# Where the products on the samples' states, memories and last cached values stand in TensorE's order

## The chip, the cores and the metric

The kernel runs on one core of one Trainium2 chip. A core has TensorE (matrix products, results into PSUM banks), VectorE, ScalarE, GpSimd and SyncE, which issues most transfers. Each engine works through its own queue in order, and an instruction waits at the head of its queue until what it needs is done. The metric is the time of one execution on the device in microseconds (us), lower is better; a kernel's time is the median of several executions.

## The reference

One inference step of one decoder layer, for two groups of tokens that share all weights: a prompt of 512 tokens and a group of samples, 8 sequences with 8 new tokens each (64 tokens). Cut to what matters here:

```
u = rms(x) * g;  proj = u @ w_in                    # z, x/B/C, dt, q, k, v, gates, og
# 1. Mamba2 scan, 16 heads in 2 groups, state h (64 x 128 per head and sequence)
y   = C.B^T-weighted sum over the new tokens  +  exp(cum) * (C @ h0)
h1  = exp(cum_last) * h0 + sum_s w_s x_s B_s
# 2. mLSTM scan, 4 heads, memory c (128 x 256) and n (128)
num = (q.k^T * D) @ v  +  s_inter * (q @ c0)
c1  = scale * c0 + sum_s w_s k_s v_s
x   = x + rms(concat(y, h_ml) @ w_out) * g
# 3. cross-attention over 256 memory rows; samples use cached keys and values
o   = softmax(q @ k_mem^T / 16) @ v_mem;  x = x + rms(o @ w_xo) * g
# 4. SwiGLU
x   = x + rms((silu(u @ w_gate) * (u @ w_up)) @ w_down) * g
```

The prompt starts from zero states. Each of the 8 samples brings its own `h0` (16 heads of 64 x 128), `c0` (4 heads of 128 x 257 with n as the last column) and cached keys and values (256 x 4 x 256 each). So `C @ h0`, `q @ c0`, `q @ k_mem^T` and `p @ v_mem` of the samples are different small products for every sample, with 8 tokens each, while everything else runs over all 576 tokens together. Outputs are both groups' tokens and all new states and memories.

## The kernel before

All data is laid out with features on the 128 partitions and tokens along the columns. A weight tile is split into a high and a low part, and each product with it is three TensorE instructions (high with high, high with low, low with high; lines 215, 216 and 218, result tiles `ps_in`, `ps_xo` and so on). Plain float32 products, such as all products on states, are two instructions each in the trace.

The order of the work on each engine is made ahead of time by a scheduler: of the instructions whose inputs it holds to be ready, it puts next the one that stands first in the program. Two constructs bend this. `with tc.issue_after(x)` puts the block's instructions of x's engine behind x in that engine's order, without a wait of its own. `with tc.high_priority(offset=3000)` lets the block's instructions go as though they stood 3000 places earlier in the program. Once made, the order is fixed, and on the chip nothing passes an instruction that waits.

The small products of the samples use a part of the array. Four samples of 8 tokens make 32 columns of the stationary operand (`cpad` and `qpad` hold one sample's 8 columns and zeros beside them), so one product fills 32 of the 128 output partitions; four products into the four quarters of one bank run side by side. The trace shows these as `128*32`, and ordinary ones as `128*128`. Products with a 64-wide stationary operand show as `128*64`. Below, a "visit" is an unbroken run of `128*32` or `32*32` instructions between two full ones.

Three places have them.

*States (lines 804 to 828).* After the prompt's scan (`ssd_prompt(0)`, `ssd_prompt(1)`) stands the samples' scan. For b = 0 to 3 the loop loads the states of samples b and 4+b into two tiles `h0` (of four, tag `t4`), multiplies them with `cpad` into the bank `psh` (line 813, tile `ps_hs`, four products over two sequences and two groups), and then, for each of the two: GpSimd scales the state in place (line 821), two products `ps_hu` make the update (line 824), VectorE adds it (line 825, collected in `added`), and SyncE stores the state (line 827). `psh` takes one of the two banks of pool `pb`, `ps_hu` the other, until `yin` (line 829) has read `psh`. Around this in time stand products of the prompt's scan: `ps_yi` (line 710; `inner[0]` to `inner[3]` are the last ones of group 0's four tiles, `inner[4]` to `inner[7]` those of group 1) and `ps_h` (line 680, `states[0]` to `states[7]`), and as filling the input projection `ps_in` and the values' projection `ps_v` (line 882). The `ps_v` products follow a list written by hand: number n is put behind a given product of the scan, the first behind `inner[2]`, those from number 133 (counted from 0) behind `states[7]`, those from 159 behind `inner[4]`. The low parts of the first two `wv` units are put behind `added[0]` in VectorE's order.

*Memories (lines 1037 to 1059).* For each half of the samples (`hb`), bank `psn` takes four products of the new tokens (line 1042, `32*32`) and then, sample by sample, a loaded `c0` (four tiles) is multiplied with `qpad` (line 1049, tile `ps_nh`, four products each), updated by `ps_cu` (line 1056) and stored. The prompt's mLSTM heads (`ps_n`, line 983) run at the same time.

*Cached values (lines 1631 to 1651 and 1663 to 1678).* `pick` is a generator: it loads eight tiles of a half's cached keys or values (two per sample, line 1627, into `kv`, four tiles at the end), multiplies each with the samples' queries or weights (line 1640; `ps_sa` for keys, `ps_os` for values), 16 products for a pair of samples in one bank, and yields between its two pairs. `sample_step(m)` runs the next part with its TensorE instructions behind m. The last use, values of the first half, falls into the loop over `xo(j, 0)`, the first half of the attention's output projection: tiles j = 0, 1, 2 do their first six of eight steps (`step(0, KT - 2)`), then the last two steps behind the last products of the prompt's attention. Those last products are `ps_ov` (lines 1612 to 1614), whose results are split by ScalarE and VectorE (lines 202 and 203) into the tiles `oh` and `ol` (the trace names them `qh` and `ql`) that the last two steps read. The first pair stands at j = 1 with no tie, the second behind tile 4. Tiles 0, 1 and 2 hold all three banks of pool `pg`, and tile 3 needs one of them back.

Of the kernel before, what the change touches and what calls it, by code (L numbers as in the profile page):

```python
# [11 lines left out]
F32 = mybir.dt.float32  # L12
# [7 lines left out]
P = 128  # L20
# [95 lines left out]
def build(nc, tc, ctx, I, O):  # L116
# [686 lines left out]
    psh = BP("ps_hs")  # L803
    added = []
    hbs = [stacks(sd, btk.rearrange("p g k -> p (g k)"), xes.rearrange("p h k -> p (h k)"), hb, 2) for hb in range(2)]
    for b in range(4):
        hns = [sd.tile([P, 16, 64], F32, name="h0", tag="t4", bufs=4) for _ in range(2)]
        for hb in range(2):
            S.dma_start(hns[hb], I["h0"][4 * hb + b])
        for g in range(2):  # L810
            for hb in (1, 0):
                q = 32 * (2 * g + hb)
                mm(psh[q:q + 32, :], cpad[:, g, 4 * hb + b, :],
                   hns[hb][:, 8 * g:8 * g + 8, :].rearrange("p h k -> p (h k)"),
                   start=b == 0, stop=b == 3, skip_group_check=True)
        for hb in range(2):
            bb, hn, (bst, xst) = 4 * hb + b, hns[hb], hbs[hb]
            bm = sd.tile([96, 256], F32R, name="bm", tag="bm", bufs=1)
            A.activation(bm, bst.bitcast(F32), AF.Copy, scale=C32("bmask")[:96, b:b + 1])
            with tc.issue_after(mults[7].ins) if b == 2 else ExitStack():  # L820
                G.tensor_tensor(hn, hn, decs[:, :, bb:bb + 1].to_broadcast([P, 16, 64]), op=ALU.mult)
            for g in range(2):
                ps = BP("ps_hu")
                mm(ps, bm[:, g * P:(g + 1) * P], xst[:, g * 512:(g + 1) * 512], start=True, stop=True)
                added.append(V.tensor_tensor(hn[:, 8 * g:8 * g + 8, :], hn[:, 8 * g:8 * g + 8, :],
                                             ps.rearrange("p (h k) -> p h k", h=8), op=ALU.add))
            S.dma_start(O["ssms"][bb], hn.rearrange("p h k -> p (h k)"))
# [106 lines left out]
    def head_norm(num, ex, n4, pool, jk):  # L934
# [19 lines left out]
        V.tensor_tensor(a, a, d, op=ALU.mult)  # L954
        return a

    for h in range(4):
        q, k = qk[:, h, :], qk[:, 4 + h, :]
        psb = MP("ps_d")
        mm(psb, sel[:68, h:h + 1].to_broadcast([68, P]), sxst[:, 0:TP], start=True, stop=True)  # L960
        qs = mp_.tile([P, 384], F32, name="qs", tag="qs", bufs=2)
        A.activation(qs, psb[:, P:TP], AF.Exp)
        G.tensor_tensor(qs, qs, q[:, P:TP], op=ALU.mult)
        dm = mp_.tile([P, 512], F32, name="dm", tag="dm", bufs=2)
        for c in range(4):
            V.scalar_tensor_tensor(dm[:, c * P:(c + 1) * P], psb[:, c * P:(c + 1) * P], CT[:, c, 64 + h:65 + h],
                                   C16("maskp"), op0=ALU.add, op1=ALU.add)
        A.activation(dm, dm, AF.Exp)
        pss = MP("ps_s")
        for c in range(4):  # L970
            mm(pss[:, c * P:(c + 1) * P], k[:, c * P:(c + 1) * P], q[:, c * P:(c + 1) * P], start=True, stop=True,
               skip_group_check=True)
        V.tensor_tensor(dm, dm, pss, op=ALU.mult)
        psk = MP("ps_k")
        for c in range(4):
            TE.transpose(psk[:, c * P:(c + 1) * P], k[:, c * P:(c + 1) * P], ident)
        kw = mp_.tile([P, 4, P], F32, name="kw", tag="kw", bufs=2)
        V.tensor_tensor(kw, psk.rearrange("p (c k) -> p c k", c=4), wendm[:, 0:4, h:h + 1].to_broadcast([P, 4, P]),
                        op=ALU.mult)
        num = mp_.tile([P, 4, 257], F32, name="num", tag="num", bufs=2)  # L980
        for c in range(4):
            psn = MP("ps_n")
            mm(psn[:, 0:257], dm[:, c * P:(c + 1) * P], vt[c][:, h, 0:257], start=True, stop=c == 0)
            if c:
                mm(psn[:, 0:257], qs[:, (c - 1) * P:c * P], cprev[:, 0:257], start=False, stop=True)
            V.tensor_copy(num[:, c, :], psn[:, 0:257])
            psc = MP("ps_c")
            mm(psc[:, 0:257], kw[:, c, :], vt[c][:, h, 0:257], start=True, stop=True)
            cn = mp_.tile([P, 258], F32, name="cst_", tag="cst_", bufs=4)
            if c == 0:  # L990
                A.copy(cn[:, 0:257], psc[:, 0:257])
            else:
                V.scalar_tensor_tensor(cn[:, 0:257], cprev[:, 0:257], scalem[:, c, h:h + 1], psc[:, 0:257],
                                       op0=ALU.mult, op1=ALU.add)
            cprev = cn
        f = head_norm(num, expnm[:, :, h:h + 1].rearrange("p c o -> p (c o)"), 4, mp_,
                      mp_.tile([P, 256], F32, name="hn_jk", tag="hn_jk", bufs=1))
        S.dma_start(O["cp"][:, h, :], cprev[:, 0:257])
        for c in range(4):
            scaled = V.tensor_scalar(num[:, c, 0:256], num[:, c, 0:256], f[:, c:c + 1], None, op0=ALU.mult)  # L1000
        for dv in range(2):
            pst = MP("ps_ht")
            for c in range(4):
                ht = TE.transpose(pst[:, c * P:(c + 1) * P], num[:, c, dv * P:(dv + 1) * P], ident)
            htc = A.copy(qk[:, 4 * dv + h, 0:TP], pst)
# [26 lines left out]
    for h in range(4):  # L1032
        TE.transpose(psk[:TS, h * P:(h + 1) * P], qk[:, 4 + h, TP:T], ident)
    kws = ms.tile([TS, 4, P], F32, name="kws")
    V.tensor_tensor(kws, psk[:TS, :].rearrange("p (h k) -> p h k", h=4),
                    wendm[:TS, 4, :].unsqueeze(2).to_broadcast([TS, 4, P]), op=ALU.mult)
    for hb in range(2):
        r = slice(32 * hb, 32 * hb + 32)
        kst, vst = stacks(ms, kws.rearrange("p h k -> p (h k)"), vts.rearrange("p h k -> p (h k)"), hb)
        psn = BP("ps_nh")  # L1040
        for h in range(4):
            mm(psn[32 * h:32 * h + 32, 0:257], ds_[r, h, r], vt[4][r, h, 0:257], start=True, stop=False,
               tile_position=(32 * hb, 32 * h), skip_group_check=True)
        for b in range(4):
            bb = 4 * hb + b
            c0 = ms.tile([P, 4, 258], F32, name="c0", tag="t4", bufs=4)
            S.dma_start(c0, I["c0"][bb])
            for h in range(4):
                mm(psn[32 * h:32 * h + 32, 0:257], qpad[:, h, bb, :], c0[:, h, 0:257], start=False, stop=b == 3,
                   skip_group_check=True)  # L1050
            km = ms.tile([96, 512], F32R, name="km", tag="km", bufs=1)
            A.activation(km, kst.bitcast(F32), AF.Copy, scale=C32("bmask")[:96, b:b + 1])
            cn = c0
# [725 lines left out]
    for j in range(8):  # L1779
        step = xo(j, 0, wx if 3 < j < 7 else None)  # L1780
        if j < 3:

            step(0, KT - 2)
            with tc.issue_after(ends[-1].ins) if j else ExitStack():
                ends.append(step(KT - 2, KT)[0])
        else:
            ends.append(step(0, KT)[0])

        if j == 1:
            next(steps, None)  # L1790
        elif j == 4:
            sample_step(ends[-1])
    kxs.close()
    u3l = SL(5, "u3l", F32R)
# [847 lines left out]
```

## Time and profile before

| | |
|---|---|
| median of 3 executions | 1073.94 us (1070.35 to 1074.08) |
| the profiled execution, its own time | 1071.59 us |
| its span, first to last instruction | 1069.8 us |
| TensorE busy | 1060.1 us, 99% |
| VectorE, ScalarE, GpSimd busy | 775.2, 616.5, 236.9 us |
| HBM read and written | 162.11 and 20.65 MB |
| granted TensorE clock | 0.999 |

The profile is of one execution. TensorE instructions overlap one another: an instruction's duration reaches past the start of the next, so the time that a product costs is read from start to start, not from its duration. A row of the timeline gives the start and the duration in us, engine, line, operation, tiles (output and inputs), shapes and the count of instructions merged into it, and in brackets the idle time before it and what ended that. A row of the chain of waits gives the start, the length and the work.

### The profile page before, as it was taken

The page shows a single profiled execution, that of the slowest core. Times are in us where ns is not written, and L with a number is a line of the kernel's source. Part 1 is how long each engine was busy: PE and PEld are TensorE (multiplying, and loading weights), DVE is VectorE, ACT ScalarE, POOL GpSimd, SP SyncE. Part 2 cuts the span into 40 slices and gives each one's busy share as a digit, 9 for nine tenths or more (in the row PEclk, how much of TensorE's full clock was granted, in tenths as well). Part 3 has the DMA queues.
Part 4 walks back from the last instruction along what each step waited for, and adds up shares of the span by engine and source line. Part 5 has one row for each costly group of instructions (what it writes and reads, how often), then busy time and mean ns, then how long its engine had stood idle before and what let it go on. Part 6 is the DMA issues. An engine that isn't in the chain of part 4 may idle for free.

```text
span 1069.8 us, 20670 instructions
## 1 busy us (share of the span) xinstructions
PE 1060.1 (99%) x8060; PEld 1006.9 (94%) x8060; DVE 775.2 (72%) x1554; ACT 616.5 (58%) x1115; POOL 236.9 (22%) x308
## 2 busy tenths in 40 slices
PE   9999999999999999999999999999999999999997
PEld 8999887778999999999999989999999999999997
DVE  6798675658887898779755556776467887787556
ACT  6778533446654557666555535545566566656654
POOL 0453643313123131010244201100011111111000
PEclk9999999999999999999999999999999999999999
DMA  6676544426654349784568775743476688578532
GB/s 209 164 172 133 160 128 171 155 69 189 192 155 139 98 128 245 289 285 139 174 208 290 269 245 177 263 119 100 128 178 141 157 191 176 117 190 187 145 120 89
DMA packets 59829, 184.10 MB, mean 172 GB/s; under 512 B 6700, under 2 KB 12204, under 8 KB 59220
## 3 DMA queue, kind: packets, MB, share of 16 engines
q1 hardware_dynamic: 43316, 139.79, 39.2%
q0 software_dynamic: 15840, 42.21, 20.8%
q8 instruction: 63, 1.03, 0.4%
q10 hardware_dynamic: 576, 0.79, 0.2%
q14 instruction: 34, 0.28, 0.1%
HBM read 162.11 MB, written 20.65 MB: 171 GB/s over the span
## 4 chain that ended last, share of the span: by engine, by line
PE 96%; DVE 2%; DMA 1%; issue 0%; ACT 0%; SPq 0%; POOL 0%; DVEq 0%; POOLq 0%
PE ps_in L218 7%; PE ps_in L215 7%; PE ps_in L216 6%; PE ps_v L882 5%; PE ps_g L2111 3%; PE ps_u L2111 3%; PE ps_g L2110 3%; PE ps_u L2112 3%; PE ps_g L2112 3%; PE ps_u L2110 3%; PE ps_dn L2110 2%; PE ps_dn L2112 2%; PE ps_dn L2111 2%; PE ps_dn L215 2%; PE ps_dn L218 2%; PE ps_o L218 2%
## 5 line engine op out<-in xcount | busy, mean ns | idle before, releaser
L215 PE MATMUL ps_in<-uh,whi 128*128 128x320 f32 (+1 forms) x544 | 162.5, 299 | 0.0
L218 PE MATMUL ps_in<-uh,wlo 128*128 128x320 f32 (+1 forms) x544 | 162.1, 299 | 0.0
L216 PE MATMUL ps_in<-ul,whi 128*128 128x320 f32 (+1 forms) x544 | 161.3, 297 | 0.0
L191 ACT CAST whi<-raw 128x1024 fp32r<-128x1024 f32 (+1 forms) x98 | 99.1, 1013 | 83.6 <-PE ps_in L216 15.9
L198 DVE TENSOR_TENSOR wlo<-raw,whi 128x512 fp32r<-128x512 f32 (+2 forms) x91 | 86.7, 953 | 54.1 <-ACT whi L191 53.0
L218 PEld LDWEIGHTS ps_in<-uh,wlo 128*128 128x128 f32 x544 | 102.1, 188 | 2.3 <-issue 1.3
L215 PEld LDWEIGHTS ps_in<-uh,whi 128*128 128x128 f32 x544 | 102.2, 188 | 1.8 <-issue 0.8
L216 PEld LDWEIGHTS ps_in<-ul,whi 128*128 128x128 f32 x544 | 102.4, 188 | 0.5
L196 POOL DMA_DIRECT2D wlo<-win x31 | 27.3, 881 | 79.8 <-ACT wlo L195 72.6
L2110 PE MATMUL ps_g<-b,whi 128*128 128x288 f32 x144 | 42.4, 295 | 0.0
L2111 PE MATMUL ps_g<-b,whi 128*128 128x288 f32 x144 | 42.3, 294 | 0.0
L2111 PE MATMUL ps_u<-b,whi 128*128 128x288 f32 x144 | 42.2, 294 | 0.0
L2110 PE MATMUL ps_u<-b,whi 128*128 128x288 f32 x144 | 42.2, 294 | 0.0
L2070 DVE TENSOR_TENSOR wlo<-sw,whi 128x1024 fp32r<-128x1024 f32 (+1 forms) x26 | 29.6, 1140 | 17.1 <-ACT whi L2069 11.8
L2083 ACT CAST whi<-rawx 128x1024 fp32r<-128x1024 f32 (+1 forms) x26 | 25.6, 986 | 26.1 <-PE ps_dn L2111 13.3
L2060 ACT CAST whi<-raw 128x1024 fp32r<-128x1024 f32 (+1 forms) x26 | 25.6, 984 | 23.0 <-PE ps_g L2111 11.8
L198 POOL TENSOR_TENSOR wlo<-raw,whi 128x512 fp32r<-128x512 f32 x17 | 29.9, 1764 | 38.1 <-ACT whi L191 38.0
L215 PE MATMUL ps_xo<-qh,whi 128*128 128x288 f32 x128 | 38.2, 301 | 0.0
L216 PE MATMUL ps_xo<-ql,whi 128*128 128x288 f32 x128 | 37.8, 297 | 0.0
L216 PE MATMUL ps_o<-mixm_l,whi 128*128 128x256 f32 (+1 forms) x128 | 37.5, 293 | 0.0
L215 PE MATMUL ps_xq<-u2h,whi 128*128 128x320 f32 (+1 forms) x128 | 37.5, 295 | 0.0
L215 PE MATMUL ps_o<-mixm_h,whi 128*128 128x256 f32 (+1 forms) x128 | 37.4, 293 | 0.0
(828 smaller groups left out, 3898.4 us busy)
## 6 DMA issues: line engine op xcount, KB each, us to landing
raw<-win SPq DMA_DIRECT2D x35, 512.0 KB, 3.9
raw<-wout SPq DMA_DIRECT2D x14, 512.0 KB, 5.9
raw<-wxq SPq DMA_DIRECT2D x13, 512.0 KB, 5.3
raw<-wgate SPq DMA_DIRECT2D x13, 512.0 KB, 4.5
raw<-wup SPq DMA_DIRECT2D x13, 512.0 KB, 5.2
wlo<-win POOLq DMA_DIRECT2D x24, 256.0 KB, 5.2
kva<-vc SPq DMA_DIRECT2D x11, 512.0 KB, 6.3
raw<-wv SPq DMA_DIRECT2D x10, 512.0 KB, 3.9
```

Source lines behind the costliest of these rows:

```text
L191: casts.append(A.copy(hi[:, :n], raw[:, :n]))
L196: accs.append(G.dma_start(lo[:, a:b], src[:, a:b], accum_op=ALU.add))
L198: e.tensor_tensor(lo[:, a:b], raw[:, a:b], hi[:, a:b].bitcast(F32), op=ALU.subtract)
L215: mm(ps, wh, ah, start=i == 0, stop=False)
L216: products.append(mm(ps, wh, al, start=False, stop=False))
L218: m = mm(ps, tiles[order[c]][1], xh(order[c], t0, n), start=False, stop=c == len(tiles) - 1)
L882: mm(ps, a, b, skip_group_check=True, **kw)
L2060: s.c1 = A.copy(s.h1[:, s.all], s.r1[:, s.all])
L2070: V.tensor_tensor(s.l2[:, s.all], sw[:, s.all], s.h2[:, s.all].bitcast(F32), op=ALU.subtract)
L2110: mm(ps, wh, b[0][k], start=start and k == 0, stop=False, skip_group_check=True)
L2111: mm(ps, wh, b[1][k], start=False, stop=False, skip_group_check=True)
L2112: m = mm(ps, wl, b[0][k], start=False, stop=k == nk - 1, skip_group_check=True)
```

## The change

The loop over states loads two pairs at a time. At b = 0 and b = 2 it loads four tiles and then issues eight products, behind `inner[1]` for the first two b and behind `states[6]` for the last two; the updates follow as before. In the memories' loop all four loads and all 16 products of a half come before the half's updates; these 16 and the four of the new tokens are put behind a product of the prompt's heads (chunk 2 of head 0 for the first half, chunk 3 of head 1 for the second), with a high priority. The first pair of the last cached values moves from tile 1 to tile 2 of the output projection, behind the sixth step of that tile, with a high priority. No product, load or evacuation is added or removed.

```diff
+    held_states = []
     for b in range(4):
-        hns = [sd.tile([P, 16, 64], F32, name="h0", tag="t4", bufs=4) for _ in range(2)]
-        for hb in range(2):
-            S.dma_start(hns[hb], I["h0"][4 * hb + b])
-        for g in range(2):
-            for hb in (1, 0):
-                q = 32 * (2 * g + hb)
-                mm(psh[q:q + 32, :], cpad[:, g, 4 * hb + b, :],
-                   hns[hb][:, 8 * g:8 * g + 8, :].rearrange("p h k -> p (h k)"),
-                   start=b == 0, stop=b == 3, skip_group_check=True)
+        if b % 2 == 0:
+            for b_ in (b, b + 1):
+                held_states.append([sd.tile([P, 16, 64], F32, name="h0", tag="t4", bufs=4) for _ in range(2)])
+                for hb in range(2):
+                    S.dma_start(held_states[b_][hb], I["h0"][4 * hb + b_])
+            for b_ in (b, b + 1):
+                for g in range(2):
+                    for hb in (1, 0):
+                        q = 32 * (2 * g + hb)
+                        with tc.issue_after((states[6] if b else inner[1]).ins):
+                            mm(psh[q:q + 32, :], cpad[:, g, 4 * hb + b_, :],
+                               held_states[b_][hb][:, 8 * g:8 * g + 8, :].rearrange("p h k -> p (h k)"),
+                               start=b_ == 0, stop=b_ == 3, skip_group_check=True)
+        hns = held_states[b]
...
+    heads_mm = {}
...
-            mm(psn[:, 0:257], dm[:, c * P:(c + 1) * P], vt[c][:, h, 0:257], start=True, stop=c == 0)
+            heads_mm[h, c] = mm(psn[:, 0:257], dm[:, c * P:(c + 1) * P], vt[c][:, h, 0:257], start=True, stop=c == 0)
...
+    AT = ((0, 2), (1, 3))
     for hb in range(2):
...
         for h in range(4):
-            mm(psn[32 * h:32 * h + 32, 0:257], ds_[r, h, r], vt[4][r, h, 0:257], start=True, stop=False,
-               tile_position=(32 * hb, 32 * h), skip_group_check=True)
+            with tc.issue_after(heads_mm[AT[hb]].ins), tc.high_priority(offset=3000):
+                mm(psn[32 * h:32 * h + 32, 0:257], ds_[r, h, r], vt[4][r, h, 0:257], start=True, stop=False,
+                   tile_position=(32 * hb, 32 * h), skip_group_check=True)
+        c0s = []
         for b in range(4):
-            bb = 4 * hb + b
-            c0 = ms.tile([P, 4, 258], F32, name="c0", tag="t4", bufs=4)
-            S.dma_start(c0, I["c0"][bb])
+            c0s.append(ms.tile([P, 4, 258], F32, name="c0", tag="t4", bufs=4))
+            S.dma_start(c0s[b], I["c0"][4 * hb + b])
             for h in range(4):
-                mm(psn[32 * h:32 * h + 32, 0:257], qpad[:, h, bb, :], c0[:, h, 0:257], start=False, stop=b == 3,
-                   skip_group_check=True)
+                with tc.issue_after(heads_mm[AT[hb]].ins), tc.high_priority(offset=3000):
+                    mm(psn[32 * h:32 * h + 32, 0:257], qpad[:, h, 4 * hb + b, :], c0s[b][:, h, 0:257], start=False, stop=b == 3,
+                       skip_group_check=True)
+        for b in range(4):
+            bb, c0 = 4 * hb + b, c0s[b]
             km = ms.tile([96, 512], F32R, name="km", tag="km", bufs=1)
...
         step = xo(j, 0, wx if 3 < j < 7 else None)
         if j < 3:
-            step(0, KT - 2)
+            mid = step(0, KT - 2)
+            if j == 2:
+                with tc.high_priority(offset=3000):
+                    sample_step(mid)
             with tc.issue_after(ends[-1].ins) if j else ExitStack():
                 ends.append(step(KT - 2, KT)[0])
         else:
             ends.append(step(0, KT)[0])
-        if j == 1:
-            next(steps, None)
-        elif j == 4:
+        if j == 4:
             sample_step(ends[-1])
```

## The prediction

> **What bounds the kernel now.** I read the page's busy time and chain first, then the chain of waits in order of time around the three changed places, then timelines of single engines.
>
> ```profile
> span 1069.8 us, 20670 instructions
> ...
> PE 1060.1 (99%) x8060; PEld 1006.9 (94%) x8060; DVE 775.2 (72%) x1554; ACT 616.5 (58%) x1115; POOL 236.9 (22%) x308
> ...
> PE 96%; DVE 2%; DMA 1%; issue 0%; ACT 0%; SPq 0%; POOL 0%; DVEq 0%; POOLq 0%
> ```
>
> TensorE is busy for 99% of the span and the chain that ends last is TensorE for 96%. So what takes a start-to-start interval out of its order shortens the kernel, and what makes its order wait lengthens it; other engines count only through such a wait. The span is 1069.8 us and the execution's own time 1071.59 us, so 1.8 us lie around it. The four executions shown (1070.35, 1071.59, 1073.94, 1074.08) have a mean of 1072.5 us: the profiled one lies 0.9 below that and 2.35 below the median of three. I make the sum against 1071.59 and add the 0.9 at the end.
>
> **What a visit costs.** The chain of waits between 613 and 640 us: start, length, work. It counts TensorE from one end to the next.
>
> ```profile
> 619.76 0.57 PE ps_os L1640 x8
> 620.32 0.33 PE ps_xo L215
> ...
> 620.91 0.55 PE ps_os L1640 x2
> 621.46 0.43 PE ps_ov L1612
> 621.90 0.56 PE ps_os L1640 x6
> 622.46 0.33 PE ps_xo L215
> ...
> 625.33 0.23 PE ps_ov L1614
> 625.55 1.00 PE ps_os L1640 x16
> 626.55 0.33 PE ps_xo L215
> 626.88 0.13 PE ps_xo L216
> ...
> 637.06 1.86 PE ps_os L1640 x32
> ```
>
> Thirty-two instructions take 1.86 us, eight 0.57: (1.86 - 0.57) / 24 = 0.054 us each, so eight are 0.43 and a run has 0.14 us that don't depend on its length. The first full product behind it takes 0.33 where an ordinary one takes 0.13: another 0.20. A visit costs 0.34 us beside its work, however short. The states and the memories pay the same:
>
> ```profile
> 170.54 0.99 PE ps_hs L813 x8
> 171.53 0.43 PE ps_v L882
> 172.21 1.84 PE ps_v L882 x8
> ...
> 199.93 0.86 PE ps_h L680 x2
> ...
> 263.55 0.57 PE ps_nh L1049 x8
> 264.12 0.63 PE ps_n L985 x2
> 264.75 0.43 PE ps_c L988 x2
> ...
> 265.74 1.44 PE ps_nh L1049 x24
> ...
> 312.94 1.87 PE ps_nh L1049 x32
> ```
>
> The 32 state instructions stand in four visits of eight. One takes 0.99 where two full instructions over the same 512 columns take 0.86 (+0.13), and the value product behind it 0.43 against 1.84 / 8 = 0.23 (+0.20). The memories' first half has two visits: 0.57 + 1.44 = 2.01 against 1.87 in one piece (+0.14), with 0.63 against 0.43 behind (+0.20). The second half is one visit already.
>
> **The change part by part.** *States, four visits to two:* 2 x 0.34 = 0.68 us less. *Memories, three to two:* 0.34 less. *Last cached values, four to one* (8, 2, 6 and 16): the runs sum to 0.57 + 0.55 + 0.56 + 1.00 = 2.68 against 1.86, 0.82 less; behind them stand 0.20 four times (620.32, 621.46, 622.46, 626.55) against once, 0.60 less; 1.42 in all. If nothing waits, 0.68 + 0.34 + 1.42 = 2.44 us go.
>
> *What the tied state products make late.* The first two sets of eight move to behind `inner[1]`. Behind them wait GpSimd's scalings, the updates, and `added[0]`, which heads the low parts of the first two value units in VectorE's order.
>
> ```profile
> 142.93 8.08 POOL L821 TENSOR_TENSOR h<-h,vt 128x1024 f32<-128x1024 f32 x4
> ```
> ```profile
> 149.13 0.68 DVE L825 TENSOR_TENSOR h<-h,ps_hu 128x512 f32<-128x512 f32 x1
> 149.73 2.36 DVE L198 TENSOR_TENSOR wlo<-raw,whi 128x1024 fp32r<-128x1024 f32 x1
> ```
> ```profile
> 153.46 1.09 PE L710 MATMUL ps_yi<-lm,xdt 128*64 128x128 f32 x16
> ...
> 155.34 0.48 PE L824 MATMUL ps_hu<-stb,bm 96*128 96x512 f32 x1
> ```
> ```profile
> 164.28 2.08 PE ps_v L882 x9
> ```
>
> At the latest `inner[1]` stays at 153.5 and the run starts behind it and its followers, where now the next other product stands, at 155.4; its first half ends 1.0 later, a scaling takes 8.08 / 4 = 2.0, product and addition about 1.0, the low part 2.4: 161.8 us. The first value product that reads it is the third, at about 164.7. Hidden with 2.9 us to spare at worst; `inner[1]` will rather come earlier, since additions and a low part leave VectorE ahead of it. The added wait has the projection's `ps_in` products to fill it. Cost taken: nothing; bound if that cover is gone: the 2.9 turned into a stall of some 1 us. SyncE's queue: the loads of b = 2, 3 wait for stores of b = 0, 1 as before, and move by at most 161.8 - 2.4 - 149.8 = 9.6 us; they have until the second run at about 201.
>
> *Memories.* All four loads of the first half have to be there at `ps_n` of chunk 2.
>
> ```profile
> 250.03 2.92 SPq L1047 DMA_DIRECT2D c<-c  x4
> ```
> ```profile
> c<-c SPq DMA_DIRECT2D x4, 516.0 KB, 7.5
> ```
>
> Issued by 252.95, landing in a median of 7.5: by about 261, and the tied run starts at 265. The first update goes behind the run instead of before it, under 1 us later on an engine order that isn't the path. Cost: nothing.
>
> *Last cached values: the run and its cover.* The run is eligible when tile 2's sixth step is through. Its place decides. Before, TensorE does the 16-run and then the last 12 of tile 2's 18 products between the last `ps_ov` and the last two steps; meanwhile the other engines split that result:
>
> ```profile
> 625.59 0.59 ACT L202 CAST qh<-ps_ov 128x512 fp32r<-128x512 f32 x1 [0.77 <-PE ps_ov L1614]
> ```
> ```profile
> 626.21 0.69 DVE L203 TENSOR_TENSOR ql<-ps_ov,qh 128x512 fp32r<-128x512 f32 x1 [0.67 <-ACT qh L202]
> ```
>
> The split ends at 626.90, 1.35 us after the product (625.55), hidden by 1.00 + 12 x 0.13 = 2.6 us of work. With the short visits gone, tile 2's 18 products are through at about 622.3 (625.55 less 2.53 for eleven `ps_ov`, less 2.28 for the three visits, plus 1.57), before most of `ps_ov`. With its priority the run goes in there, and then `ps_ov` is the last thing TensorE has: tile 3 has no bank, so the last two steps wait for the split, 1.35 us, less the three products on the other half's result (0.39): a stall of 0.96 us takes the place of the visits. The fourth load:
>
> ```profile
> L1627 SPq DMA_DIRECT2D kvb<-vc x1: 928/928/928, 614.7 to 614.7; - x1
> ...
> DMA to landing us min/median/max: 9.0/9.0/9.0
> ```
>
> It lands at 623.7; the run's last quarter starts at 622.3 + 1.3 = 623.6: 0.1 us of waiting. So this place gives 1.42 - 0.96 - 0.1 = 0.36. The next four loads start when the run frees their tiles, by 624.3, and with 9.0 us land by 633.3, ahead of the second pair at 637.
>
> **The sum:** 0.68 + 0.34 + 0.36 = 1.4 us; 1071.59 - 1.4 = 1070.2, and with the 0.9 for the middle of the executions **1071.1 us**.
>
> **The rivals.** *The cover stays* (20%): the run stands behind `ps_ov`, and its 1.86 us cover the 1.35. All 2.44 us go: 1071.59 - 2.4 + 0.9 = 1070.1. For it: `ps_ov` comes first in the program and its inputs may be held ready before tile 2 is through. Against it: the run has the priority.
>
> *The run stays broken* (12%; the change does not do what it says): the four loads are issued one behind the other, the last lands at 623.7, and a priority starts the run with those it has. With two visits the place saves 1.42 - 0.34 = 1.08, and part of the cover returns: 1.4 to 2.1 us in all, 1070.4 to 1071.1.
>
> *Slower: the second set of updates collides with group 1* (13%). Four scalings and eight additions, spread from 170.5 to 207.3 before, cannot start before `states[6]` at 200.8 and fall just ahead of `inner[4]`, behind which value products from number 159 are tied: if VectorE has its `lm` late, TensorE stands.
>
> ```profile
> 147.15 2.06 DVE L703 TENSOR_TENSOR lm<-lm,cbs 128x512 f32<-128x512 f32 x1
> ...
> 152.01 0.68 DVE L703 TENSOR_TENSOR lm<-lm,cbs 128x512 f32<-128x512 f32 x1
> ...
> 205.98 1.28 DVE L825 TENSOR_TENSOR h<-h,ps_hu 128x512 f32<-128x512 f32 x2
> ...
> 211.28 0.69 DVE L703 TENSOR_TENSOR lm<-lm,cbs 128x512 f32<-128x512 f32 x1 [0.16 <-ACT lm L702]
> ```
> ```profile
> 216.01 1.02 PE ps_yi L710 x15
> ```
>
> `lm` is ready at 212.0 and used at 216.0: 4.0 us of slack. At worst six more additions come first (6 x 0.68 = 4.1), and both multiplications L703 take 2.06, as the one did during GpSimd's scalings, instead of 0.68 (+2.8): 6.9 - 4.0 = 2.9 us of stall, 1071.59 - 1.4 + 2.9 + 0.9 = 1074.0. It decides from 4.0 us of delay, and makes the kernel slower from 5.4. Against it: VectorE idles for part of that stretch, and the scheduler may put `lm` first. [...]
>
> The remaining 10% is an order that shifts somewhere else, in either direction.
>
> **How the numbers follow.** Forecast 45%, and the cases above. Forecast alone, with executions scattering by 2 around their middle: 1069 to 1073.2. The range goes down to the case with the cover, less that scatter and 1.5 for a shifted order (1066.5), and up to the slow case with 1.5 (1075.5). About 0.5% (5.4 us) is what a measurement of this kernel can tell from no change. No worked case reaches it: faster by more needs the scatter or a shifted order on top of the 2.4 (10% of forecast, 20% of the cover's case, half the rest: 14%); slower by more needs the collision to go on into `inner[5]` (a third of its case) or the other half of the rest (9%); within it 77%.
>
> **What would show it.** Eleven visits in these places become five (16 and 16 instructions, 40 and 40, and 32), at 0.34 us each; TensorE at `inner[2]` and the first value product without a gap; a gap of about 1 us between the last `ps_ov` and the last two steps of tile 0 if the run stands ahead of `ps_ov`, none if behind; `ps_yi` near 216 without idle time. Wrong would be a wait inside a run, a run in pieces, or a gap at `inner[4]`.

## The result

The changed kernel takes 1078.26 us (median of 6 executions, 1077.22 to 1079.87); the kernel before, executed beside it, 1071.6 us (1070.2 to 1074.1). The ratio is 1.0063 with an interval of 1.0052 to 1.0074: slower by 0.6%, outside the range of the prediction, on the side that it gave the least chance. The profiled execution took 1078.48 us.

The page of the changed kernel (span, busy time, share of the chain that ended last):

```profile
span 1076.7 us, 20662 instructions
...
PE 1060.7 (99%) x8060; PEld 1009.0 (94%) x8060; DVE 777.1 (72%) x1554; ACT 616.8 (57%) x1115; POOL 239.7 (22%) x308
...
PE 94%; DVE 3%; DMA 1%; issue 0%; ACT 0%; POOL 0%; SPq 0%; DVEq 0%; POOLq 0%
```

TensorE has the same 8060 instructions and 0.6 us more busy time, but the span is 6.9 us longer: its order stands still where it did not before. What it waited for (waits of TensorE, with us in total, times, longest):

```profile
PE ps_yi L710 <- DVE lm L703: 3.5, 1, 3.5
...
PE ps_xo L218 <- DVE wlo L198: 0.8, 1, 0.8
PE ps_rb L1871 <- DVE px_r L1864: 0.6, 1, 0.6
PE ps_ht L1011 <- DVE num L1007: 0.6, 1, 0.6
PE ps_hu L830 <- DVE h L831: 0.5, 1, 0.5
PE ps_o L215 <- DVE tmp L1157: 0.4, 1, 0.4
```

Of these only `ps_rb` stood before the change too (0.6 us). The runs themselves came out as forecast; the chain of waits of the changed kernel shows all five:

```profile
152.71 1.85 PE ps_hs L818 x16
...
204.43 1.85 PE ps_hs L818 x16
...
271.01 0.57 PE ps_nh L1051 x8
271.57 1.87 PE ps_nh L1059 x32
...
317.44 1.87 PE ps_nh L1059 x32
...
632.06 1.86 PE ps_os L1652 x32
```

Sixteen instructions on the states (eight products) take 1.85 us where two visits of eight took 2 x 0.99, and 32 on the last cached values 1.86 where four visits took 2.68.

Where the time went is read from the start of the same product in both traces, after minus before. In the changed kernel it is 0.0 at 120 us, +5.4 at 250, +7.1 at 420 and +6.8 at 660, and stays there. So the states' place costs 5.4 us, the memories' place 1.7, and the last cached values give 0.3 back. This is the largest piece, in the chain of waits:

```profile
150.65 1.02 PE ps_yi L710 x16
...
156.08 2.16 DVE lm L700 x8
...
158.49 2.21 DVE lm L703
160.70 0.60 DVE h L831
161.29 3.41 DVE wlo L198 x2
164.71 0.61 DVE lm L703
...
165.36 1.76 PE ps_yi L710 x13
```

The last row is `inner[2]`. Its second `lm` multiplication (164.71) stands on VectorE behind the first addition to a state and the low parts of the first two value units, and the multiplication ahead of them takes 2.21 us. TensorE's projection products, the filling, end at 160.8; the value products are tied behind `inner[2]`; so TensorE has nothing left. Before the change the two multiplications for `inner[2]` followed each other on VectorE with nothing between:

```profile
160.82 1.29 DVE L703 TENSOR_TENSOR lm<-lm,cbs 128x512 f32<-128x512 f32 x2
```

In the changed kernel GpSimd scales four states beside the first of them:

```profile
154.41 8.08 POOL L827 TENSOR_TENSOR h<-h,vt 128x1024 f32<-128x1024 f32 x4
```

The gap costs more than its own 3.46 us. The stretches of 1 us behind it (busy time of each engine, then the granted TensorE clock, DMA share and GB/s):

```profile
164.00:165.00 1.00, 0.00 (x0) 0.00 (x0) 1.00 (x2) 0.00 (x0) 0.00 (x0) 1.00 0.44 94
165.00:166.00 1.00, 0.64 (x6) 0.64 (x8) 1.00 (x3) 0.00 (x0) 0.00 (x0) 0.56 0.90 319
166.00:167.00 1.00, 1.00 (x14) 1.00 (x12) 0.30 (x1) 0.00 (x0) 0.00 (x0) 0.50 0.86 279
167.00:168.00 1.00, 1.00 (x8) 0.51 (x5) 0.61 (x1) 0.75 (x1) 0.00 (x0) 0.50 0.98 332
168.00:169.00 1.00, 1.00 (x7) 0.99 (x7) 0.80 (x2) 0.69 (x2) 0.00 (x0) 0.73 0.90 365
169.00:170.00 1.00, 1.00 (x6) 0.79 (x5) 1.00 (x2) 0.00 (x0) 0.00 (x0) 1.00 0.38 139
```

The clock is halved from 165.1, just before TensorE is back at 165.36, until 168.5: a mean of 0.56 over 165 to 166 us is 0.12 us at full and 0.88 at half clock, and 0.73 over 168 to 169 is 0.54 us at half. The clock lost to TensorE's work is 0.50 x 0.64 + 0.50 + 0.50 + 0.27 = 1.6 us, and it can be seen in the work: `inner[2]` takes 1.76 us where `inner[1]` took 1.02. From start to start the waits cost a little more than the idle time shown: the update product starts 0.79 us after the one ahead of it instead of 0.15, and `inner[2]` 3.92 us after that one instead of 0.34. The states' place adds up to 0.6 + 3.6 (waits) + 1.6 (clock) - 0.7 (two visits) = 5.1 of the 5.4 us.

### The profile page after: what moved, and what is told of

The parts are those of the page before. It is cut to its first block, busy times and chain, and to the rows that moved or that the text cites. A ratio compares the mean times of both kernels' runs of the same rounds, so it can differ in the third digit from the quotient of the medians.

```text
span 1076.7 us, 20662 instructions
## 1 busy us (share of the span) xinstructions
PE 1060.7 (99%) x8060; PEld 1009.0 (94%) x8060; DVE 777.1 (72%) x1554; ACT 616.8 (57%) x1115; POOL 239.7 (22%) x308
## 4 chain that ended last, share of the span: by engine, by line
PE 94%; DVE 3%; DMA 1%; issue 0%; ACT 0%; POOL 0%; SPq 0%; DVEq 0%; POOLq 0%
PE ps_in L215 6%; PE ps_in L218 6%; PE ps_in L216 6%; PE ps_v L888 5%; PE ps_g L2124 3%; PE ps_u L2124 3%; PE ps_g L2123 3%; PE ps_u L2125 3%; PE ps_g L2125 3%; PE ps_u L2123 3%; PE ps_dn L2123 2%; PE ps_dn L2125 2%; PE ps_dn L2124 2%; PE ps_dn L215 2%; PE ps_dn L218 2%; PE ps_dn L216 2%
## 5 line engine op out<-in xcount | busy, mean ns | idle before, releaser
L198 DVE TENSOR_TENSOR wlo<-raw,whi 128x512 fp32r<-128x512 f32 (+2 forms) x91 | 88.0, 968 | 56.3 <-ACT whi L191 55.4
L198 POOL TENSOR_TENSOR wlo<-raw,whi 128x512 fp32r<-128x512 f32 x17 | 30.0, 1764 | 38.4 <-ACT whi L191 38.3
L218 PE MATMUL ps_xo<-qh,wlo 128*128 128x288 f32 x128 | 37.1, 296 | 0.8 <-DVE wlo L198 0.8
```

Of the source, the lines that this page charges most:

```text
L198: e.tensor_tensor(lo[:, a:b], raw[:, a:b], hi[:, a:b].bitcast(F32), op=ALU.subtract)
L218: m = mm(ps, tiles[order[c]][1], xh(order[c], t0, n), start=False, stop=c == len(tiles) - 1)
```

## The experiments

Theory A says that the loss is this order on VectorE, set off by the tied state products. Theory B says that longer runs or their ties cost by themselves. The prediction's collision at `inner[4]` is a third, and theory C puts a part of the loss on the memories. The table sets every kernel against the kernel before: the ratio with its interval, and from its profile by how much the start of the same products fell behind in each stretch (us later at its end than at its beginning; negative is gained). A start at 120 us, ahead of everything that was changed, already lies between 1.4 us earlier and 0.8 later than in the profile of before, so single executions scatter by that much, and of the profiles only the stretches are compared.

| kernel | ratio | 120-250 us | 250-420 | 420-660 |
|---|---|---|---|---|
| the change | 1.0063 [1.0052, 1.0074] | +5.4 | +1.7 | -0.3 |
| without states | 1.0006 [0.9997, 1.0015] | 0.0 | +1.7 | -0.9 |
| states alone | 1.0058 [1.0046, 1.0071] | +7.0 | +0.1 | 0.0 |
| memories alone | 1.0018 [1.0009, 1.0027] | 0.0 | +1.7 | +0.1 |
| last cached values alone | 0.9996 [0.9987, 1.0005] | 0.0 | 0.0 | -1.0 |
| first run of states alone | 1.0071 [1.0054, 1.0089] | +7.7 | 0.0 | 0.0 |
| second run of states alone | 0.9994 [0.9981, 1.0007] | +0.3 | +0.1 | +1.9 |
| the change, first run behind `inner[0]` | 1.0009 [1.0001, 1.0017] | +0.3 | +1.4 | -0.4 |
| the change, low parts later | 1.0047 [1.0032, 1.0062] | +4.8 | +1.6 | -0.3 |
| the change, low parts and scalings later | 1.0023 [1.0010, 1.0036] | +3.9 | +1.4 | -0.7 |
| memories, first half alone | 0.9998 [0.9989, 1.0006] | 0.0 | -0.3 | +0.2 |
| memories, second half alone | 0.9994 [0.9985, 1.0004] | 0.0 | -0.2 | +0.1 |
| memories, two updates later | 1.0035 [1.0022, 1.0049] | 0.0 | +2.6 | +1.5 |
| that, with the cached values | 1.0029 [1.0018, 1.0039] | 0.0 | +2.6 | -0.5 |
| memories' first half, cached values | 0.9990 [0.9982, 0.9999] | 0.0 | -0.4 | -0.2 |

### One part at a time

*Without the states' part* (the changed kernel, loop over states as before):

```diff
-    held_states = []
     for b in range(4):
-        if b % 2 == 0:
...
+        hns = [sd.tile([P, 16, 64], F32, name="h0", tag="t4", bufs=4) for _ in range(2)]
```

> The change without its states part: memories and last cached values as changed, states as before. Theory A (VectorE's order): the loss is the 3.46 us in which TensorE stands ahead of inner[2], behind the first addition and two low parts that VectorE has between the two lm multiplications; that order comes from the tied state products alone, so without them the place runs without a gap. The memories' 0.34 and what the last cached values keep (visits -1.42, a wait of 0.8 for a low part behind the later pair) leave 0.5 to 1 us less than before: ratio 0.999 to 1.0. Theory B (the runs themselves or their ties cost, at the memories or the cached values): slower than before by 1 us or more. Theory C (small stalls near 389 and 394 us of the changed kernel, 0.6 and 0.4 us, are set off by the memories' ties): they stay here and eat the gain, ratio 1.0 to 1.001.

Measured 1071.59 us, ratio 1.0006. The gap ahead of `inner[2]` is gone, and with it the 5.4 us of that place. But no gain is left: the gaps near 383 and 387 us are there, and the memories' place takes 1.7 us as theory C has it.

*The states' part alone* (the first hunk of the change, nothing else):

```diff
+                        with tc.issue_after((states[6] if b else inner[1]).ins):
...
```

> The states part alone; memories and last cached values as before. Theory A: the whole loss is here, the gap ahead of inner[2] as in the changed kernel (some 3.5 us) and what follows in the two scans; 3.5 to 7 us more than before, ratio 1.0035 to 1.0065. Theory B: no more than 1 us more than before, and no gap ahead of inner[2]. If the 1.5 us that the changed kernel loses between 345 and 390 us belong to the memories, this one stands at about +5; if to the states' shift, at +6 to +7.

Measured 1077.03 us, ratio 1.0058, with the same gap. It loses more in its place (7.0) than the changed kernel does there (5.4), with the same code, and the clock says why:

```profile
163.00:164.00 1.00, 0.00 (x0) 0.00 (x0) 1.00 (x2) 0.00 (x0) 0.00 (x0) 0.72 0.27 53
...
169.00:170.00 1.00, 1.00 (x4) 0.75 (x3) 0.21 (x1) 0.00 (x0) 0.71 (x1) 0.50 0.16 53
170.00:171.00 1.00, 1.00 (x5) 0.81 (x4) 0.00 (x0) 0.00 (x0) 0.29 (x1) 0.86 0.07 29
```

Here the halved clock lasts from 163.4 to 170.3, 6.8 us instead of 3.4. Most of the 1.6 us between the two is this: TensorE works at half clock from 164.53 to 170.3, which loses 2.9 us instead of 1.6.

*The memories' part alone* (the second hunk):

```diff
+            with tc.issue_after(heads_mm[AT[hb]].ins), tc.high_priority(offset=3000):
```

> The memories part alone. By the prediction's own count one visit less: -0.34 us, a ratio of 0.9997, which five rounds can hardly tell from 1. Theory C (the ties of the memories set off the small stalls near 389 and 394 us): +0.5 to +1 us, and the stalls are in this trace. Theory A: they are not.

Measured 1072.83 us, ratio 1.0018: theory C, and the forecast of the memories falls. Its waits of TensorE:

```profile
PE ps_ht L1005 <- DVE num L1001: 0.6, 1, 0.6
PE ps_o L215 <- DVE tmp L1151: 0.3, 1, 0.3
```

Until 340 us it is 0.4 ahead: the visit is saved. Then come the transposes of head 2, before and in this kernel:

```profile
344.16 0.38 PE L1004 MATMUL ps_ht<-c,num 128*128 128x128 f32 x2
```
```profile
347.29 0.38 PE L1005 MATMUL ps_ht<-c,num 128*128 128x128 f32 x2
```

They start 4.0 us later when the 0.88 that this execution was ahead are taken off; head 3 follows them, its normalization ends late, the projection's products that stood beside it are used up, and TensorE waits. From start to start of the same products these two waits cost 0.94 and 0.60 us, more than their idle time.

*The last cached values alone* (the third hunk):

```diff
+                with tc.high_priority(offset=3000):
+                    sample_step(mid)
```

> The last cached values alone: four visits become one. If nothing waits, -1.42 us (ratio 0.9987). In the changed kernel a wait of 0.8 us for a low part stands behind the second pair of cached values; if the later first pair makes that part late, it is here too and -0.5 is left (ratio 0.9995). If the run stood ahead of the last products on the prompt's attention, a wait of 0.96 us would stand before the last two steps of tile 0; in the changed kernel it stands behind them, so none is expected.

Measured 1070.45 us, ratio 0.9996; by the profile 1.4 us are saved and 0.5 given back behind the second pair; another 0.4 are lost at 680 us, behind the table's last stretch and in a part that this kernel doesn't change. In the changed kernel the wait behind the second pair is 0.8 us, and its chain leads through a low part to a load:

```profile
637.16 6.33 DMA raw<-wxo
...
643.51 1.05 ACT whi L191
...
644.65 1.24 DVE wlo L198
...
645.93 0.40 PE ps_xo L218
```

The load is issued as early as before, against the start of the same products, but it lands later. The median time from issue to landing of these loads, in the changed kernel between 632 and 640 us and in the kernel before between 618 and 636:

```profile
raw<-wxo SPq DMA_DIRECT2D x2, 512.0 KB, 6.0
```
```profile
raw<-wxo SPq DMA_DIRECT2D x2, 512.0 KB, 4.6
```

One run frees four tiles at once, so four loads of cached values of 512 KB each start together (632.69 to 634.07 us) and stand beside them; before they came two by two (620.38 and 622.51, 626.18 and 626.62). That the four slow the others is the reading that fits; no run spaced them out.

### Which of the two runs of states

*Only the first two sets together behind `inner[1]`*, and *only the last two behind `states[6]`*:

```diff
+            bs = (0, 1) if b == 0 else (b,)
...
+                        with tc.issue_after(inner[1].ins) if b == 0 else ExitStack():
```
```diff
+            bs = (2, 3) if b == 2 else (b,)
...
+                        with tc.issue_after(states[6].ins) if b == 2 else ExitStack():
```

> Only the first two sets of state products together behind inner[1]; the last two sets, memories and last cached values as before. Theory A: the gap ahead of inner[2] as in the changed kernel, 3 to 4 us over before less one visit of 0.34 (ratio 1.0025 to 1.0035). Collision: nothing of the loss here.

> Only the last two sets of state products together behind states[6]; the rest as before. Theory A: no gap ahead of inner[2]; one visit less, -0.34 us, if the later updates cost nothing. The offset of the changed kernel grows by 1 to 2 us between 200 and 240 us; if that is the second run's doing (collision), this kernel is slower than before by 1 to 2 us (ratio 1.001 to 1.002).

The first run has the whole loss (ratio 1.0071) and more than was expected, for here the halved clock lasts 6.8 us too (162.7 to 169.5). The second is at 0.9994: no collision. By the profile its place stands at +0.3 us, one visit saved and a gap of 0.4 at `inner[3]`; the +1.9 behind 420 us are mostly a wait of 1.3 for a load of cached values in the profiled execution, in a part that this kernel doesn't change.

*The change with its first run behind `inner[0]`*:

```diff
-                        with tc.issue_after((states[6] if b else inner[1]).ins):
+                        with tc.issue_after((states[6] if b else inner[0]).ins):
```

> The changed kernel with its first run of state products tied behind inner[0] instead of inner[1]; still one run of 16. Theory A: the first addition and the low part go back to their place ahead of inner[1], where the projection's products fill TensorE, and inner[2] has nothing in front of it; the gap is gone and the kernel takes what the prediction said, 0.5 to 2 us less than before (ratio 0.998 to 0.9995), as far as the second run does not cost. Theory B: a run of 16 costs wherever it stands: ratio 1.004 or more. Collision at inner[4]: only the gap goes, 1 to 2 us over before stay (ratio 1.001 to 1.002) and they stand between 200 and 240 us.

Measured 1072.44 us, ratio 1.0009: one name in a tie is worth 5.8 us. Both multiplications for `inner[2]` follow each other on VectorE, 0.65 us each, and TensorE has its products up to `inner[2]`:

```profile
159.41 0.68 DVE L831 TENSOR_TENSOR h<-h,ps_hu 128x512 f32<-128x512 f32 x1
160.00 1.29 DVE L703 TENSOR_TENSOR lm<-lm,cbs 128x512 f32<-128x512 f32 x2
```
```profile
161.17 0.24 PE ps_hu L830
161.41 1.03 PE ps_yi L710 x16
```

It is no test of the run's length: behind `inner[0]` the run stands in two pieces of eight (140.3 and 144.1 us), as before.

### Taking the gap apart

*The change with the low parts of the first two value units behind the second multiplication for `inner[2]`*:

```diff
-            with tc.issue_after(added[0].ins) if g == 0 and u < 2 else ExitStack():
+            with tc.issue_after(mults[5].ins) if g == 0 and u < 2 else ExitStack():
```

> The changed kernel with one edit in VectorE's order: the low parts of the first two units of the values' weights stand behind the second lm multiplication of the third tile (mults[5]) instead of behind the first addition to a state. All products, loads and runs stay. Theory A: the multiplication no longer waits for the two low parts (3.49 us), so it ends at about 162 to 163 instead of 165.3; the gap ahead of inner[2] falls from 3.46 to at most 1 us, and the time by 2 to 3 us, unless the first value products then wait for their low part (read by the third one, about 1.5 us behind inner[2]). Theory B (the tied runs themselves cost): no change in time from the changed kernel, ratio 1.006.

Measured 1076.66 us, ratio 1.0047. The gap falls from 3.46 to 1.2 us, and the order on VectorE shows what is left of it, the slow multiplications:

```profile
157.31 2.21 DVE L703 TENSOR_TENSOR lm<-lm,cbs 128x512 f32<-128x512 f32 x1
159.45 0.67 DVE L831 TENSOR_TENSOR h<-h,ps_hu 128x512 f32<-128x512 f32 x1
160.04 1.82 DVE L703 TENSOR_TENSOR lm<-lm,cbs 128x512 f32<-128x512 f32 x1
161.78 2.35 DVE L198 TENSOR_TENSOR wlo<-raw,whi 128x1024 fp32r<-128x1024 f32 x2
```

The time fell by 1.6 us, less than the 2 to 3 expected and than the 2.3 of the gap, since 1.2 us come back at 174 us, where an update product waits for an addition. And the clock was halved even so:

```profile
160.00:162.00 2.00, 0.55 (x3) 0.27 (x5) 2.00 (x3) 0.51 (x1) 1.31 (x1) 1.00 0.00 0
162.00:164.00 2.00, 2.00 (x23) 1.75 (x24) 2.00 (x2) 0.49 (x1) 0.00 (x0) 0.84 0.03 8
164.00:166.00 2.00, 2.00 (x7) 1.67 (x7) 2.00 (x5) 0.00 (x0) 0.00 (x0) 0.50 0.92 268
```

*The same, with GpSimd's scalings of the first two sets behind that multiplication too* (a copy of one column on GpSimd marks the place):

```diff
+                if len(mults) == 6:
+                    marks.append(G.tensor_copy(sd.tile([P, 1], F32, name="lm1"), lm[:, 0:1]))
...
-            with tc.issue_after(mults[7].ins) if b == 2 else ExitStack():
+            with tc.issue_after(mults[7].ins) if b == 2 else tc.issue_after(marks[0].ins) if b < 2 else ExitStack():
```

> The changed kernel, run of 16 behind inner[1] as it is, with two edits: the low parts of the first two units of the values' weights stand behind the second lm multiplication of the third tile (as in the run with that edit alone, which left a gap of 1.19 us), and GpSimd's scalings of the first two sets start only behind that multiplication too. Theory A (what stands between the lm multiplications on VectorE, and the scalings that slow them): both multiplications take 0.68 us instead of 2.21 and 1.82, inner[2] has no gap, and the TensorE clock stays at 1.0 where it fell to 0.5 behind the gap in the changed kernel. The kernel is then within 1.5 us of the one with the run behind inner[0] (ratio 1.0 to 1.002), unless the later additions make inner[3] late. Rival (a full run behind inner[1] costs by itself): ratio stays at 1.004 or more with no gap there.

Measured 1074.81 us, ratio 1.0023. With no scaling beside them the two multiplications and the two low parts take 3.6 us (1.29 + 2.35), where they took 6.4 in the changed kernel (2.21 + 3.49 + 0.68, with an addition between):

```profile
157.48 1.29 DVE L703 TENSOR_TENSOR lm<-lm,cbs 128x512 f32<-128x512 f32 x2
158.68 2.35 DVE L198 TENSOR_TENSOR wlo<-raw,whi 128x1024 fp32r<-128x1024 f32 x2
```

`inner[2]` has no gap, with the full run of 16 behind `inner[1]`, so the run itself is not what costs there. But the delay has moved one tile on. Now the scalings (161.04 to 169.65) make the next additions late, and `inner[3]` waits 1.5 us for its `lm` behind another wait of 0.7; the clock, expected to stay full, is halved from 173 to 176.5 us. So the kernel stays some 1.5 us above the one with the run behind `inner[0]` (1.0023 against 1.0009), a little more than expected.

### The memories

*The first half alone*, and *the second half alone* (the other half as before):

```diff
+            if hb == 0:
+                c0 = c0s[b]
+            else:
+                c0 = ms.tile([P, 4, 258], F32, name="c0", tag="t4", bufs=4)
```
```diff
+            if hb == 1:
+                c0 = c0s[b]
```

> The memories part for the first half of the samples alone; the second half, one visit already, as before. If the second half's ties cause the loss of the memories part (+1.7 us by its profile), this one saves 0.3 to 0.5 us; if the first half's do, it stays at +1 to +1.7 us, and head 2's transposes are late here too.

> The memories part for the second half of the samples alone; the first half as before. The first half alone gained 0.33 us by its profile and left no gap; both halves together lost 1.7. If the loss is the second half's ties (one visit before and after, so no visit to gain), this one loses 1 to 2 us (ratio 1.001 to 1.002) with gaps near 383 and 387.5 and head 2's transposes some 3 us late. If the loss needs both halves, it stands at 0 to +0.3 us.

The first half saves 0.34 us by its profile, exactly one visit; the second saves 0.2 (0.9994, so no loss of the expected kind); neither has a gap. That the second half's ties cost is refuted: the loss needs both. The transposes of head 2 fit this. They are late by 2.0 us with the first half's part, by 1.9 with the second's and by 4.0 with both. That the products beside the last normalization cover 2 us and not 4 is the reading that fits; no run tried a delay between.

*Both halves, with the additions to the second half's last two memories behind head 2's normalization*:

```diff
-                V.scalar_tensor_tensor(cn[:, h, :], c0[:, h, :], es[:, h, 8 * bb + 7:8 * bb + 8], ps[:, 0:258],
+                with tc.issue_after(heads_sc[2].ins) if hb and b >= 2 else ExitStack():
+                    V.scalar_tensor_tensor(cn[:, h, :], c0[:, h, :], es[:, h, 8 * bb + 7:8 * bb + 8], ps[:, 0:258],
...
```

> The memories part alone, with the additions to the last two memories of the second half put behind the normalization of head 2 in VectorE's order. In the memories' part alone head 2's transposes stood 3.1 us later than before, head 3 behind them 2 to 3 us later, and the projection's products that should cover the last normalization were used up: gaps of 0.58 and 0.35 us at 383 and 387.5. Theory C (memory additions that come earlier push head 2's normalization back in the order): with this edit head 2's transposes are back at their place of before, the gaps are gone and the kernel saves what the longer run saves, 0.3 to 0.5 us (ratio 0.9990 to 1.0000). If the ties on TensorE are what costs, it stays at 1.001 to 1.0025.

Measured 1075.95 us, ratio 1.0035, worse. Up to 370 us it is 0.5 us ahead, head 2's transposes are no longer late (343.72 us, 1.3 earlier than before when the 0.8 that this execution was behind are taken off), and the two gaps are gone. But another order comes out behind, and in it TensorE waits for VectorE to empty a bank of the projection:

```profile
PE ps_o L215 <- DVE tmp L1152: 2.9, 1, 2.9
```

*The same with the last cached values as changed*:

```diff
+                with tc.high_priority(offset=3000):
+                    sample_step(mid)
```

> States as before; memories as changed with the additions to the last two memories of the second half behind head 2's normalization; last cached values as changed. If each saves by itself what the runs so far bear out (0.3 to 0.5 and 0.4 to 0.9 us), 0.7 to 1.4 us less than before, ratio 0.9987 to 0.9994; if the wait of 0.8 us behind the second pair of cached values comes back, 0.9995.

Measured 1074.73 us, ratio 1.0029: the 2.9 us wait is here too. A miss of the same kind.

### What can be kept

*Memories of the first half and last cached values as changed; states and second half as before*:

```diff
+                if hb == 0:
+                    tie.enter_context(tc.issue_after(heads_mm[AT[hb]].ins))
+                    tie.enter_context(tc.high_priority(offset=3000))
...
+                with tc.high_priority(offset=3000):
+                    sample_step(mid)
```

> The two parts that gained by their profiles, together: memories of the first half (-0.33 us) and the last cached values (-0.6 to -0.9 us); states and second half as before. If they add, 0.9 to 1.2 us less than before, ratio 0.9989 to 0.9992; if the wait for a low part behind the second pair of cached values is 0.8 instead of 0.3 us, 0.7 less (0.9993). No other gap.

Measured 1070.98 us against 1072.31 of the kernel before, ratio 0.9990 [0.9982, 0.9999]. It is the one of the fifteen versions whose interval lies below 1, and it ends just there; the ratio stands for some 1.1 us. Its profile shows 0.5 us gained from 120 us on, and a gap of 0.4 at 615 us, where TensorE waits for GpSimd ahead of `ps_pt`, that was not expected. So the gain is small, and not shown piece by piece.

## Why the prediction was wrong

*Right: what a visit costs.* Two visits of eight state instructions against one of 16, 1.98 us against 1.85, differ by 0.13, the 0.14 of the prediction; the memories' first half alone gained 0.34, as counted; the last cached values gained 1.4, as counted (1.42). The visits fell as it said.

*Wrong: what the tied state products make late.* The step said that the first run "starts behind it and its followers", that the low part is done by 161.8 and read at 164.7, and closed with "The added wait has the projection's `ps_in` products to fill it. Cost taken: nothing". It followed one consumer, the third value product. It missed that the addition and the low parts stand in VectorE's order, in front of whatever comes there next. Before the change that was the second multiplication for `inner[1]`, and the rows for it were quoted: L703 2.06, L825, L198 2.36, L703. TensorE had projection products beside it. Tied behind `inner[1]`, the same group moves in front of the second multiplication for `inner[2]`, where the projection's products end (161.8 us before, 160.8 after) and the value products are tied behind. The bound for lost cover, "some 1 us", took the slack of the wrong reader. The gap was 3.46 us, 0.5 stood ahead of it, and 1.6 followed in clock, of which the prediction had no term. The run behind `inner[0]` and the two edits to the order show it: with the low parts moved away 1.2 us of the gap are left, and with the scalings moved away too it is gone.

*Right mechanism, wrong place: the slower rival.* A set of updates that makes `lm` late, with multiplications of 2.06 beside GpSimd's scalings, is what happened, but with the first run at `inner[2]` and not with the second at `inner[4]`. At `inner[4]` nothing waits; the second run alone measures 0.9994, with 0.4 us at `inner[3]`.

The multiplications took 2.21 and 1.82 us beside scalings and 0.65 without, the two low parts 3.49 against 2.35. The addition to a state at 160.62 us of the changed kernel stands beside the same scalings and takes 0.67, as the one at 165.63 does without. With the scalings moved behind them the two multiplications take 1.29 together, so in these runs the scalings slow them; by what means, and why not the addition, no run shows.

*Wrong: the memories.* "The first update goes behind the run instead of before it, under 1 us later on an engine order that isn't the path. Cost: nothing." For each half alone that holds. For both together the order of head 2 moves by 4.0 us, and 2.0 us are lost against the 0.34 saved; 1.5 of them stand at the two waits, counted from start to start, and the rest in steps of up to 0.3 us that were not traced further. Delaying the additions to two memories on VectorE made head 2 early again and took the two gaps away, so their place in VectorE's order moves it; but it made another wait of 2.9 us, so what each half adds to the loss of both stays open.

*Last cached values.* The rival was right: the run stands behind the last `ps_ov` (631.57 and 632.06), its 1.86 us cover the split, and the forecast stall of 0.96 is not there. In its place a load that lands later costs up to 0.8 us. So the value for the place came out near the forecast (0.3 to 1.0 gained, 0.36 forecast) by luck: the loss that was counted isn't there, and one that was not counted is.

*The 0.9 for the middle of the executions* came from four of them; of the six beside the changed kernel the median is 1071.6, the profiled one's own time, so this term was scatter.

## What to carry to other kernels

A tie moves more than the tied products: list what hangs on them on every engine, find the instruction that now stands behind that group on each, and ask whether TensorE still has untied work when it waits for it (that untied value products would have covered the gap, no run tried). A stall's price is its length plus the time at a lower clock that can follow, here 1.6 us behind a gap of 3.5 and 2.9 behind one of 3.4. Gains of 0.34 us per visit are real, but a change that keeps the visits and moves an order written by a scheduler can lose ten times that in one place; take the parts that leave the order alone.

## What was not expected of the hardware

The TensorE clock halved behind some gaps, for 3.41 us (165.1 to 168.5 in the changed kernel) or 6.8 us (163.4 to 170.3 with the states alone), then returned to 1.0; 0.50 is the only lower value in the traces of the kernels before and after. There the stretches of the clock's record, up to the one that the end of the profile cuts off, are whole multiples of 3.413 us: in the changed kernel, 160.43 us at full clock, 3.41 at half and 904.53 at full are 47, 1 and 265 of them; in the kernel before, 1061.55 us at full are 311.

With the states alone a gap of about the same length (3.4 us against 3.5) cost more. In the 3.413 us ahead of the clock's fall TensorE was idle for 2.85 us and in the 3.413 behind it for 1.08, and the clock stayed halved for 6.8 us; in the changed kernel it was 3.22 and 0.24, and 3.41. That the idle time behind the fall is what kept the clock down is the reading that fits; no run varied it alone.

The length of a gap alone does not tell whether the clock falls behind it. Behind gaps of 0.5 and 1.2 us with one product between (the run with the low parts later) it was halved: TensorE is idle for 1.45 of the 2 us from 160 to 162, and the clock stands at 0.50 from 164 to 166. Behind a gap of 2.87 us, in the memories' kernel with two updates later, it was not:

```profile
388.00:390.00 2.00, 0.39 (x4) 0.19 (x2) 1.96 (x3) 0.00 (x0) 0.01 (x1) 1.00 0.00 0
390.00:392.00 2.00, 0.74 (x5) 0.74 (x6) 2.00 (x4) 0.70 (x2) 0.00 (x0) 1.00 0.00 0
392.00:394.00 2.00, 2.00 (x16) 2.00 (x15) 1.92 (x4) 1.27 (x2) 1.53 (x2) 1.00 0.67 219
```

What decides there these runs don't tell.
